# Six raw weight buffers and three pairs of split ones, in place of four and four

## The chip, the cores and the metric

The kernel runs on one core of one Trainium2 chip. The time is device microseconds from the first to the last instruction of the program, as a median over runs. Five engines work side by side, each with an instruction stream of its own: TensorE (PE in the profile; its weight loads are shown as PEld), VectorE (DVE), ScalarE (ACT), GpSimd (POOL) and SyncE (SP), which here issues nearly all loads from memory. They wait for one another through semaphores.

## The reference

The program is a forward pass over 256 tokens of width 1024 in fp32, through two blocks of two layers each. In outline:

```python
for l in range(2):                                # first block
    p = x @ w_in[l]
    h = concat(gmlp(p), diff_attention(p), pool(p)) @ w_out[l]
    x = layer_norm(ALPHA * x + h)
    f = swiglu(x, w1, w3, w2) if l == 0 else moe_ffn(x, router, w1, w3, w2)
    x = layer_norm(ALPHA * x + f)
for l in range(2):                                # second block
    z = rmsnorm(x) @ w_in_2[l]
    br = stack([sparse_attention(z), retention(z), conv_module(z)])
    x = x + sum(gate(z) * (br @ w_branch[l])) @ w_out_2[l]
    x = x + relu(rmsnorm(x) @ w_ff1[l]) ** 2 @ w_ff2[l]

def swiglu(x, w1, w3, w2): return (silu(x @ w1) * (x @ w3)) @ w2
def moe_ffn(x, ...):                              # top 2 of 8 experts, each a swiglu of width 3584
    return sum(gates[:, e] * swiglu(x, w1[e], w3[e], w2[e]) for e in range(8))
```

Every weight is read once. Nearly all the work is products of 256 tokens, or of the tokens that an expert has, with these weights.

## The kernel before

An fp32 product is made of three faster ones: a weight is split into a high part `wh` and a low part `wl`, an activation likewise, and high·high, low·high and high·low are summed in PSUM (line 84; line 945 for the experts).

**A unit** (`unit`, lines 166 to 212) is 2048 columns of weights on 128 partitions, 1 MB. It takes a raw buffer from the pool `pw` (tag "raw") and a buffer each for `wh` and `wl` from the pool `ph`. SyncE issues its load (line 188), ScalarE copies it into `wh` (line 165, which rounds), and VectorE subtracts `wh` from the raw weights into `wl` (line 166). There are 532 of these subtractions. A raw buffer is free for another load when the subtraction is done, a pair is free when TensorE's last product on it is done. A few other tensors take a raw buffer as well (the compression weights of the sparse attention, the merged branches).

**How units are called.** The dense products (`run_b`, `run_a`, `pipe`) load one unit ahead of the one that is multiplied. A dense unit has 24 products of 512 columns. At the head of a layer and in the output projection, two or three units are held at once, and all of them are multiplied with the first 128 tokens, then all with the second 128 (`tmajor`), while the normalization of one token tile runs.

**The experts** (`expert`, `moe`, `stream`) run from about 440 to 1470 us of the span and load 336 units, two to three ahead of their work. The branch that these inputs take, `few`, has two parts. In part 1, to about 840 us, three experts run interleaved: one with a full tile of 128 gathered tokens and a half one, so that a unit has 20 products, and two with a half tile of 64 tokens, so that a unit has 8. I call these heavy and light units. A round has 18 units, in runs of heavy ones and of light ones, and between the runs the products of the two up matrices are turned (`uT`, lines 992 and 999) and split for the down matrix (`uh`, `ul`, `uhl`). In part 2 one expert with one full tile runs at a time, 12 products to a unit, 6 units to a round.

**What sets the order.** The program is written as generators that are woven together, but each engine's final order is made by a scheduler at build time. It plays the program through with durations of its own and gives each engine the instructions in the order in which they could start there; an instruction that needs a buffer becomes possible when the buffer is free in that play. So the numbers of buffers (`bufs`, lines 402 and 403) move instructions on ScalarE, VectorE and, here and there, on TensorE and SyncE.

Of the kernel before, what the change touches and what calls it, by code (L numbers as in the profile page):

```python
# [75 lines left out]
class Acc:  # L76
    """a PSUM region that n matmuls accumulate in; fresh: the first one clears the bank"""
# [11 lines left out]
def weave(main, fill):  # L89
    """emit main; ("wait", us) in it is covered by that much tensor-engine work of fill, ("until", f) by  # L90
    what it takes to make f() true"""
    for kind, t in main:
        while kind == "until" and not t():
            next(fill)
        while kind == "wait" and t > 0:
            r = next(fill, None)
            if r is None:
                break
            if r[0] == "work":
                t -= r[1]  # L100
# [7 lines left out]
class Gated:  # L108
    """a generator that comes to a halt ahead of job n until ready()"""
# [16 lines left out]
def blend(a, b, every):  # L126
    """a, with a step of b emitted after each `every` us of it"""
    due = 0.0
    for r in a:
        yield r  # L130
        if r[0] == "work":
            due += r[1]
        while due >= every:
            due -= every
            next(b, None)


class Model:
# [29 lines left out]
    def unit(self, src, ks, c0, n, layout=None, scale=None):  # L168
        """rows of the k-tiles ks, columns c0.. of a weight, in two float32r parts [128, k, n]; scale: a factor
        [128, 1] for the rows of each k-tile"""  # L170
# [11 lines left out]
        else:  # L182
            i = 0
            while i < nk:
                j = i + 1
# [4 lines left out]
                i = j  # L190
# [5 lines left out]
        elif scale:  # L196
            i = 0
# [16 lines left out]
    def run_b(self, specs, x, tiles=(0, 1), tmajor=False, after=None):  # L214
        """token-layout products. specs: (src, ks, c0, n, {t: [(Acc, column slice)]}, layout);
        tmajor: all units for one token tile, then for the other; after[t]() is emitted behind tile t,
        after[t, i]() behind unit i of it"""
        nc = self.nc

        def emit(sp, u, t):  # L220
            h, l = u
            w = 0
            for kk, k in enumerate(sp[1]):
                xh, xl = x(k, t)
                for acc, cs in sp[4][t]:
                    acc.mm(nc, xh, h[:, kk, cs])
                    acc.mm(nc, xh, l[:, kk, cs])
                    acc.mm(nc, xl, h[:, kk, cs])
                    w += 3 * 0.000428 * (cs.stop - cs.start)
            return ("work", w)  # L230

        load = lambda sp: self.unit(*sp[:4], *sp[5:])
        if tmajor:
            us = [load(sp) for sp in specs]
            for t in tiles:
                for i, (sp, u) in enumerate(zip(specs, us)):
                    yield emit(sp, u, t)
                    if after and (t, i) in after:
                        after[t, i]()
                if after and t in after:  # L240
                    after[t]()
        else:
            nxt = load(specs[0]) if specs else None
            for i, sp in enumerate(specs):
                u, nxt = nxt, (load(specs[i + 1]) if i + 1 < len(specs) else None)
                for t in tiles:
                    yield emit(sp, u, t)

    def pipe(self, jobs):
        """token-layout products of one job after the other, units loaded ahead across them.  # L250
        jobs: (units, x, begin, end), units = [(src, ks, c0, n, layout, scale)] of n columns in all,
        begin() ahead of the products, end(banks) behind them; yields ("job", index) ahead of each"""
# [21 lines left out]
    def specs_b(self, src, nk, c0, n, tiles=(0, 1), layout=None, order=None, per=None,  # L274
                scale=None):
        """units and banks of out[t] = x[t] @ src[:, c0:c0+n]"""
# [7 lines left out]
    def run_a(self, src, c0, n, parts, x, nk=8, layout=None):  # L284
        """feature-layout product; parts: (bank, rows, column offset in bank, column offset in the unit)"""
# [19 lines left out]
    def feat(self, src, c0, nf, x, out):  # L305
        """nf tiles of 128 features, two to a bank: [128, f%2, tok]"""
# [3 lines left out]
    def to_feat(self, src, t, xh, xl):  # L310
        """src [128 tok, 1024] -> xh/xl[:, k, t*128:...] split transposed"""
# [20 lines left out]
    def bcast_row(self, dst, src):  # L332
        """DRAM vector [n] to all partitions of dst [128, n]"""
# [3 lines left out]
    def warm(self, func, after):  # L337
        """has the scalar engine's table for func loaded ahead of its use, once after [128, n] is there"""
# [6 lines left out]
    def rsqrt(self, v, eps):  # L345
        """v = (v + eps) ** -0.5 for a few columns, without a table of the scalar engine"""
# [33 lines left out]
    def project(self, src, orders, x, post, scale=None, first=None):  # L380
        """out = x @ src [., 1024]; the last three units go tile by tile, post(t, banks) behind each tile.
        orders: lists of k-tiles that make up units; first() is emitted behind the first products, self.early()
        ahead of the last"""
# [15 lines left out]
    def setup(self, ctx):  # L399
        tc, nc = self.tc, self.nc  # L400
        self.alpha = 4.0 ** 0.25
        self.pw = ctx.enter_context(tc.tile_pool(name="pw", bufs=4))
        self.ph = ctx.enter_context(tc.tile_pool(name="ph", bufs=4))
# [56 lines left out]
    def mix1(self, l, xt, tr1):  # L460
        """-> the generator of the output projection, begun. tr1() emits the transposes of the second token tile"""
# [156 lines left out]
    def attn1(self, qT, kT, v, bt, neglam, yth, ytl):  # L618
# [37 lines left out]
        def values(hp):  # L656
            """[token, (t, head of the pair, feature)]"""
# [118 lines left out]
    def ln_out(self, gen, g, b):  # L776
        """drains a projection into a layer norm; -> (transposed x, emitter of its second tile)"""
# [23 lines left out]
    def route(self, xt, rw):  # L801
        """by slot: gates, positions of the tokens (far off where they are not routed), expert, token count"""
# [51 lines left out]
        # slots: the experts by their number of tokens, most first. Of the 512 places, no more than three can  # L854
        # have over 128, and the last none over 64
# [49 lines left out]
    def gather(self, g, parts, xh, xl):  # L905
        """x^T of the tokens that the one-hots g[t] [128 tok, 256 or 512] pick, in two parts. parts: the
        destination [128, 8, n] of each part for columns of g, as (first column, n, high, low)"""
# [18 lines left out]
    def expert(self, tiles, w, acc):  # L926
        """the phases of acc[tok] += gate[tok] * swiglu of the gathered tiles, put back on their tokens: a list of
        (jobs, then), jobs = [(unit arguments, tensor-engine work on the unit, what follows it)]"""
# [4 lines left out]
        def mms(tile, src, k):  # L933
            """(stationary operand, part of the weights, rows of the product)"""
# [5 lines left out]
        def products(tile, src, ks, u, targets):  # L940
            """targets: (Acc, columns of the unit); ks: k-tiles of src"""
# [121 lines left out]
    def stream(self, jobs, ahead=2):  # L1063
        """emits jobs (unit arguments or None, work on the unit, what follows), units loaded ahead of their work"""
        queue, units = [], []

        def pull():
            """on to the next job with a unit, which is loaded"""
# [15 lines left out]
    def moe(self, xt, rw, w1, w3, w2, g2, b2):  # L1084
# [19 lines left out]
        def place(slots):  # L1104
            """slots: (slot, first position, half) of the tiles, in 512 columns -> tiles"""
# [43 lines left out]
        def phases(rounds):  # L1149
            """jobs of rounds of experts whose phases alternate; the last products of a phase follow the first of  # L1150
            the next"""
# [25 lines left out]
        def run(plan):  # L1177
            """plan: (groups of tiles to place, rounds of experts); a group is placed ahead of its first round"""
# [53 lines left out]
    def residual_norm(self, t, banks, dst):  # L1232
        """xn = x + banks; dst = rmsnorm(xn) * gamma, for token tile t"""
# [14 lines left out]
    def rms_out(self, gen, gamma, name=None):  # L1248
        """drains a projection into the residual and its norm; -> the norm by tile or, with a name, transposed and
        the emitter of its second tile"""  # L1250
# [28 lines left out]
    def mix2(self, l, xt, tr1):  # L1279
# [4 lines left out]
        # parameters that belong on partitions  # L1284
# [28 lines left out]
        # gated convolution input, in token layout first  # L1313
# [22 lines left out]
        # retention operands in token layout  # L1336
# [21 lines left out]
        def gates(n, c, dst):  # L1358
            """tanh of half the gate logits of branch n, columns 512 c.. -> dst() [128, t, 512]"""
# [8 lines left out]
        def branch(n, c, layout=None, scale=None):  # L1368
            """merged += 2 * gate * projection of branch n, columns 512 c.."""
# [21 lines left out]
        def turn(c):  # L1391
            """the transposed merged columns 512 c.. in two parts"""
# [88 lines left out]
    def ret_gate(self, w, tok, gr, ys):  # L1481
        """gr = 2 silu(g)"""
# [8 lines left out]
    def retention(self, r0, qk, vr, gr, dec, ys):  # L1491
# [20 lines left out]
        def values(t):  # L1512
            """[token, (head, feature)], normalized over the features"""
# [44 lines left out]
    def gelu_tanh(self, dst, src):  # L1558
        """0.5 x (1 + tanh(sqrt(2/pi) (x + 0.044715 x^3)))"""
# [40 lines left out]
    def nsa_in(self, l, w, full, par, fold, N):  # L1600
        """keys, values, gates and queries; tile j of the queries holds head j of both groups"""
# [6 lines left out]
        # windows of keys and values to compress; the positional part is one more window  # L1608
# [74 lines left out]
    def nsa(self, N, ys):  # L1683
# [62 lines left out]
        # compressed scores of all heads  # L1746
# [33 lines left out]
        # selection and window attention: with 256 tokens both see every earlier key  # L1780
# [110 lines left out]
```

## Time and profile before

| | |
|---|---|
| runs | 2375.16, 2378.10, 2379.86 us, median 2378.1 |
| profiled execution | span 2376.3 us; its own time beside the span is not given |
| TensorE busy | 2285.2 us (96%), 11444 products |
| VectorE busy | 1770.3 us (74%), of which `wl` of line 166: 1200.9 us in 532 |
| ScalarE busy | 1410.7 us (59%), of which `wh` of line 165: 1003.5 us in 532 |
| DMA | 585.10 MB, mean 246 GB/s |

The table adds up over stages with different limits, so it is read with the busy time by stretch. A product that is waiting in TensorE's pipeline counts as busy, so that its idle time is the surer number. Where an instruction in the order of time has a bracket behind it, its engine stood idle that long before it, and the bracket names what ended the wait.

### The profile page before, as it was taken

The numbers are of one execution on the slowest core, as the hardware profiler recorded it, in microseconds if no ns is written. First come the engines' busy times: TensorE is split into PE (matmuls) and PEld (weight loads), VectorE is DVE, ScalarE is ACT, GpSimd is POOL, SyncE is SP. The second block draws the span as 40 slices with busy tenths as digits, with TensorE's granted clock in tenths as the row PEclk, the third lists the DMA queues.
The fourth block names the chain that finished last, engine by engine and source line by source line (L and its number), as shares of the span: only waits on it lengthen the run. The fifth ranks groups of instructions, "written<-read, shape, count | busy, mean of one in ns | idle before, by whom it ended". The sixth has DMA issues, their size and how long they took to land. (4 is left out here: it accounts for less than half of the span.)

```text
span 2376.3 us, 29764 instructions
## 1 busy us (share of the span) xinstructions
PE 2285.2 (96%) x11444; PEld 1854.5 (78%) x11444; DVE 1770.3 (74%) x1907; ACT 1410.7 (59%) x1532; POOL 109.3 (5%) x154
## 2 busy tenths in 40 slices
PE   7999999799999989999999998899999999999998
PEld 6788886577777768887888776787888888888887
DVE  4665465798888998889888887898566459966653
ACT  5554354577777767677777775547554344764542
POOL 2100010100000000000000000100100001010000
PEclk9999999899999999999999999899999999999999
DMA  9456560699999989999999998553655554555552
GB/s 289 171 194 181 177 206 22 230 337 342 343 341 315 322 317 350 348 361 353 375 336 368 358 347 302 190 179 116 213 183 182 195 184 131 183 168 199 181 187 75
DMA packets 266967, 585.10 MB, mean 246 GB/s; under 512 B 10513, under 2 KB 21189, under 8 KB 266560
## 3 DMA queue, kind: packets, MB, share of 16 engines
q1 hardware_dynamic: 260880, 565.48, 68.7%
q0 software_dynamic: 5936, 17.64, 2.4%
q8 instruction: 91, 1.49, 0.3%
q14 instruction: 60, 0.49, 0.1%
HBM read 580.43 MB, written 2.64 MB: 245 GB/s over the span
## 5 line engine op out<-in xcount | busy, mean ns | idle before, releaser
L166 DVE TENSOR_TENSOR wl<-raw,wh 128x2048 fp32r<-128x2048 f32 (+2 forms) x532 | 1200.9, 2269 | 391.6 <-ACT wh L165 389.4
L165 ACT ACTIVATE wh<-raw 128x2048 fp32r<-128x2048 f32 (+2 forms) x532 | 1003.5, 1895 | 515.4 <-PE lin L84 145.1
L945 PE MATMUL lin<-wh,ring 128*128 128x512 f32 x1680 | 556.1, 392 | 0.0
L945 PE MATMUL lin<-wl,ring 128*128 128x512 f32 (+1 forms) x1008 | 399.0, 396 | 9.4 <-DVE wl L166 9.3
L945 PEld LDWEIGHTS lin<-wh,ring 128*128 128x128 f32 x1680 | 315.4, 188 | 81.2
L945 PEld LDWEIGHTS lin<-wl,ring 128*128 128x128 f32 (+1 forms) x1008 | 171.3, 170 | 63.2 <-DVE wl L166 23.2
L84 PE MATMUL lin<-wh,hh 128*128 128x512 f32 x352 | 142.0, 404 | 0.0
L84 PE MATMUL lin<-wl,hh 128*128 128x512 f32 x352 | 138.4, 393 | 2.3 <-DVE wl L166 2.3
L84 PE MATMUL lin<-wh,hl 128*128 128x512 f32 x352 | 138.0, 393 | 0.1
L945 PE MATMUL y<-wl,uh 128*128 128x512 f32 x336 | 107.6, 401 | 3.8 <-DVE wl L166 3.8
L1427 DVE SCALAR_TENSOR_TENSOR ro<-conv,ro 128x256 f32<-128x256 f32 x240 | 105.5, 474 | 0.4
L945 PE MATMUL y<-wh,ul 128*128 128x512 f32 x336 | 104.3, 391 | 0.0
L945 PE MATMUL y<-wh,uh 128*128 128x512 f32 x336 | 104.1, 390 | 0.0
L84 PE MATMUL lin<-wh,h2h 128*128 128x512 f32 x256 | 101.1, 395 | 0.0
L84 PE MATMUL lin<-wl,h2h 128*128 128x512 f32 x256 | 99.9, 390 | 0.2
L84 PE MATMUL lin<-wh,h2l 128*128 128x512 f32 x256 | 99.3, 390 | 0.2
L84 PE MATMUL lin<-wh,xah 128*128 128x512 f32 (+1 forms) x240 | 87.7, 366 | 0.7 <-ACT xah L165 0.6
L84 PE MATMUL lin<-wh,xal 128*128 128x512 f32 (+1 forms) x240 | 86.7, 364 | 0.0
L84 PE MATMUL lin<-wl,xah 128*128 128x512 f32 (+1 forms) x240 | 86.6, 361 | 0.0
L84 PEld LDWEIGHTS lin<-wl,hh 128*128 128x128 f32 x352 | 66.8, 190 | 16.1 <-DVE wl L166 3.2
L84 PEld LDWEIGHTS lin<-wh,hh 128*128 128x128 f32 x352 | 66.8, 190 | 15.7 <-issue 1.3
L84 PEld LDWEIGHTS lin<-wh,hl 128*128 128x128 f32 x352 | 66.7, 189 | 14.7 <-DVE hl L166 0.4
(543 smaller groups left out, 3781.0 us busy)
## 6 DMA issues: line engine op xcount, KB each, us to landing
raw<-in_moe_w SPq DMA_DIRECT2D x336, 1024.0 KB, 6.8
raw<-in_w_in SPq DMA_DIRECT2D x70, 1024.0 KB, 5.2
raw<-in_w_ff SPq DMA_DIRECT2D x64, 1024.0 KB, 5.2
raw<-in_ffn_w SPq DMA_DIRECT2D x32, 1024.0 KB, 5.1
raw<-in_w_out SPq DMA_DIRECT2D x12, 1024.0 KB, 8.2
raw<-in_w_branch SPq DMA_DIRECT2D x8, 1024.0 KB, 5.9
raw<-in_w_out SPq DMA_DIRECT2D x8, 512.0 KB, 8.3
raw<-in_w_branch SPq DMA_DIRECT2D x8, 512.0 KB, 6.4
```

Source lines behind the costliest of these rows:

```text
L84: nc.tensor.matmul(o, lhsT=lhsT, rhs=rhs, start=(self.i == 0 and self.fresh), stop=(self.i == self.n - 1), skip_group_check=True)
L165: self.nc.scalar.activation(h, src, AF.Copy)
L166: self.nc.vector.tensor_sub(l, src, h.bitcast(F32))
L945: nc.tensor.matmul(a.ap[:rows], lhsT=lhsT, rhs=u[part][:, kk, cs], start=(a.i == 0), stop=(a.i == a.n - 1), skip_group_check=True)
L1427: nc.vector.scalar_tensor_tensor(acc[:, f], uT[:, f, k:k + 256], cw[:, f, k:k + 1], acc[:, f], op0=OP.mult, op1=OP.add)
```

## The change

The pool of raw buffers gets six buffers in place of four, and the pool of split ones three of each tag in place of four. A raw buffer has 8 KB per partition and a pair 16 KB, so that the memory in use is the same. All else in the diff is comments that are taken out; no line number moves.

```diff
-        self.pw = ctx.enter_context(tc.tile_pool(name="pw", bufs=4))
-        self.ph = ctx.enter_context(tc.tile_pool(name="ph", bufs=4))
+        self.pw = ctx.enter_context(tc.tile_pool(name="pw", bufs=6))
+        self.ph = ctx.enter_context(tc.tile_pool(name="ph", bufs=3))
```

Every engine has the same instructions before and after, up to waits; what differs is the order. Two places show how.

The first is VectorE in part 1 of the experts, where a run of light units begins: `wl_4055`, `wl_4071`, `wl_4104` and `wl_4119` are the low parts of the first four light units of the run, `wl_4138` is that of the first heavy unit behind them, `ysum` the sum of a light expert's products, `ul` and `uhl` low parts of activations. Before:

```order
L166 TENSOR_TENSOR wl_4055<-raw_4053,wh_4054 128x2048
L980 TENSOR_TENSOR sa_3992<-sa_3992,lin_4016 128x512
L166 TENSOR_TENSOR wl_4071<-raw_4069,wh_4070 128x2048
L1022 COPY ysum_3382<-y_4059 128x512
L1022 COPY ysum_3382<-y_4060 128x512
L166 TENSOR_TENSOR wl_4104<-raw_4102,wh_4103 128x2048
L166 TENSOR_TENSOR ul_4091<-uT_4085,uh_4090 128x512
L166 TENSOR_TENSOR wl_4119<-raw_4117,wh_4118 128x2048
L166 TENSOR_TENSOR uhl_4099<-uT_4094,uhl_4099 128x4x64
L971 TENSOR_TENSOR sa_4131<-lin_4108,sa_4131 64x512
L166 TENSOR_TENSOR wl_4138<-raw_4136,wh_4137 128x2048
```

With the change:

```order
L980 TENSOR_TENSOR sa_3992<-sa_3992,lin_4016 128x512
L166 TENSOR_TENSOR wl_4055<-raw_4053,wh_4054 128x2048
L166 TENSOR_TENSOR wl_4071<-raw_4069,wh_4070 128x2048
L1022 COPY ysum_3382<-y_4059 128x512
L1022 COPY ysum_3382<-y_4060 128x512
L166 TENSOR_TENSOR ul_4091<-uT_4085,uh_4090 128x512
L166 TENSOR_TENSOR uhl_4099<-uT_4094,uhl_4099 128x4x64
L166 TENSOR_TENSOR wl_4104<-raw_4102,wh_4103 128x2048
L166 TENSOR_TENSOR wl_4119<-raw_4117,wh_4118 128x2048
L971 TENSOR_TENSOR sa_4131<-lin_4108,sa_4131 64x512
L166 TENSOR_TENSOR wl_4138<-raw_4136,wh_4137 128x2048
```

The multiplication of line 980 between the first two subtractions goes ahead of them, and `ul` and `uhl`, each of which stood behind a subtraction, go ahead of the third one, so that subtractions stand two by two.

The second is VectorE at the head of the dense feed-forward network, while the normalization ahead of it still runs (`r`, `st`, `mv`, lines 360 to 372): `wl_1090`, `wl_1096`, `wl_1102` and `wl_1194` are the low parts of its first four units, `xal` the low part of the first token tile. Before:

```order
L360 SCALAR_TENSOR_TENSOR r_1060<-x_86,prj_824 128x512
L166 TENSOR_TENSOR wl_1096<-raw_1094,wh_1095 128x2048
L166 TENSOR_TENSOR xal_1033<-tr_1034,xah_1032 128x4x128
L166 TENSOR_TENSOR xal_1033<-tr_1041,xah_1032 128x4x128
L362 BN_STATS st_1061<-r_1060 128x6
L360 SCALAR_TENSOR_TENSOR r_1060<-x_86,prj_826 128x512
L166 TENSOR_TENSOR wl_1102<-raw_1100,wh_1101 128x2048
L362 BN_STATS st_1061<-r_1060 128x6
L166 TENSOR_TENSOR wl_1194<-raw_1192,wh_1193 128x2048
```

With the change:

```order
L360 SCALAR_TENSOR_TENSOR r_1060<-x_86,prj_824 128x512
L166 TENSOR_TENSOR wl_1090<-raw_1088,wh_1089 128x2048
L166 TENSOR_TENSOR xal_1033<-tr_1034,xah_1032 128x4x128
L166 TENSOR_TENSOR xal_1033<-tr_1041,xah_1032 128x4x128
L362 BN_STATS st_1061<-r_1060 128x6
L360 SCALAR_TENSOR_TENSOR r_1060<-x_86,prj_826 128x512
L166 TENSOR_TENSOR wl_1096<-raw_1094,wh_1095 128x2048
L362 BN_STATS st_1061<-r_1060 128x6
L166 TENSOR_TENSOR wl_1102<-raw_1100,wh_1101 128x2048
```

Each unit's subtraction stands where the next unit's stood; that of the first unit stood farther ahead before, and that of the fourth, `wl_1194`, comes farther behind now.

## Rows read from the trace of the kernel before

**Rows 1.** The page, busy time, share of the span and instructions of TensorE.
```profile
PE 2285.2 (96%) x11444; PEld 1854.5 (78%) x11444; DVE 1770.3 (74%) x1907; ACT 1410.7 (59%) x1532; POOL 109.3 (5%) x154
```

**Rows 2.** Busy time by stretch (length, TensorE, weight loads, VectorE, ScalarE, GpSimd, clock, DMA).
```profile
140.00:200.00 60.00, 60.00 (x275) 49.85 (x274) 33.90 (x23) 29.61 (x23) 0.00 (x0) 1.00 0.62 203
440.00:840.00 400.00, 387.00 (x1766) 286.83 (x1764) 351.63 (x279) 298.07 (x266) 0.00 (x0) 1.00 0.95 333
840.00:1470.00 630.00, 619.76 (x2800) 502.73 (x2800) 554.96 (x365) 450.16 (x318) 0.00 (x0) 1.00 0.97 350
```

**Rows 3.** The page, issues of the experts' loads (count, size, median us to landing).
```profile
raw<-in_moe_w SPq DMA_DIRECT2D x336, 1024.0 KB, 6.8
```

**Rows 4.** Order of time, 512 to 531 (start, duration, engine, line, tiles, idle before and releaser).
```profile
512.13 1.90 ACT L165 ACTIVATE wh<-raw 128x2048 fp32r<-128x2048 f32 x1
...
515.20 2.29 DVE L166 TENSOR_TENSOR wl<-raw,wh 128x2048 fp32r<-128x2048 f32 x1
...
515.78 0.39 PE L945 MATMUL lin<-wh,ring 128*128 128x512 f32 x1
...
516.01 0.40 PE L945 MATMUL lin<-wl,ring 128*64 128x512 f32 x1
...
516.21 3.72 ACT L165 ACTIVATE wh<-raw 128x2048 fp32r<-128x2048 f32 x2 [2.18 <-PE lin L945]
...
520.37 1.28 DVE L1022 COPY ysum<-y 128x512 f32<-128x512 f32 x2
...
521.56 2.28 DVE L166 TENSOR_TENSOR wl<-raw,wh 128x2048 fp32r<-128x2048 f32 x1
...
523.76 0.68 DVE L166 TENSOR_TENSOR ul<-uT,uh 128x512 fp32r<-128x512 f32 x1
...
524.36 2.28 DVE L166 TENSOR_TENSOR wl<-raw,wh 128x2048 fp32r<-128x2048 f32 x1
...
525.20 0.39 PE L945 MATMUL lin<-wl,ring 128*64 128x512 f32 x1
...
526.56 0.41 DVE L166 TENSOR_TENSOR uhl<-uT,uhl 128x256 fp32r<-128x256 f32 x1
...
527.01 0.68 DVE L971 TENSOR_TENSOR sa<-lin,sa 64x512 f32<-64x512 f32 x1
...
527.73 2.29 DVE L166 TENSOR_TENSOR wl<-raw,wh 128x2048 fp32r<-128x2048 f32 x1
...
530.08 0.73 PE L945 MATMUL y<-wl,uh 128*128 128x512 f32 x2 [0.34 <-DVE wl L166]
```

**Rows 5.** Waits, 447 to 840 (engine and line, what for, total, times, longest).
```profile
PE y L945 <- DVE wl L166: 7.9, 16, 1.2
...
PE lin L945 <- DVE wl L166: 2.9, 6, 0.7
```

**Rows 6.** Waits, 840 to 1470.
```profile
ACT wh L165 <- DMA raw<-in_moe_w: 118.9, 120, 4.5
...
PE lin L945 <- DVE wl L166: 6.4, 13, 1.0
...
PE y L945 <- DVE wl L166: 1.1, 2, 0.9
```

**Rows 7.** Waits of SyncE's load queue, 840 to 1470.
```profile
SPq L188 <- DVE wl L166: 460.9, 195, 4.9
```

**Rows 8.** DMA, 840 to 1470 in 40 slices, GB/s.
```profile
GB/s 272 367 330 355 350 371 323 353 333 372 341 356 361 364 363 352 378 324 376 366 369 377 317 338 355 327 376 374 373 376 347 350 359 307 357 361 373 345 381 238
```

**Rows 9.** Order of time, 121 to 127, VectorE and TensorE.
```profile
125.64 2.28 DVE L166 TENSOR_TENSOR wl<-raw,wh 128x2048 fp32r<-128x2048 f32 x1
...
126.83 0.39 PE L84 MATMUL lin<-wl,xah 128*128 128x512 f32 x1
```

**Rows 10.** Order of time, 1582 to 1587, VectorE and TensorE.
```profile
1582.03 4.62 DVE L166 TENSOR_TENSOR wl<-raw,wh 128x1024 fp32r<-128x1024 f32 x4
...
1584.67 0.28 PE L84 MATMUL q<-hh,wl 128*128 128x256 f32 x1
```

## The prediction

> **What bounds the kernel now.** I read the busy shares first, then the busy time by stretch, then the list of waits in the two stretches where TensorE is not full, and last the order of time around one place of each kind. TensorE is busy 96% of the span [rows 1]. By stretch the picture splits in two. In a dense stretch TensorE works 60.00 of 60 us while the DMA engines are busy 0.62 [rows 2]: there a weight load that starts earlier can give nothing. In the mixture of experts TensorE lacks 400.00 − 387.00 = 13.0 us between 440 and 840, where three experts run interleaved (part 1), and 630.00 − 619.76 = 10.2 us between 840 and 1470, where one tile of tokens runs at a time (part 2); the DMA share is 0.95 and 0.97 [rows 2]. A weight load of 1 MB takes 6.8 us there [rows 3]. So all that a deeper load queue could save lies in these two stretches: 23 us at the very most, since TensorE's work stays the same. The granted clock is 1.00 in all three stretches [rows 2], so no term of the sum is a clock.
>
> A weight passes two rings. A raw buffer is taken when its load is issued and given back by VectorE's subtraction, and a pair (high, low) is taken by ScalarE's copy and given back by TensorE's last product on it. The change lengthens the first ring by two and shortens the second by one, so the price hangs on which ring is late where.
>
> **Part 1: the pair ring is the late one.** In each round the units run as heavy ones (20 products) and light ones (8 products). Before a run of light units the splits must be ahead, since a light unit is eaten in 8 × 0.23 = 1.84 us (a product follows the one before by 0.23 us, as 516.01 does 515.78) while VectorE needs 2.29 us for one subtraction [rows 4]. The same rows show how the ring stands: ScalarE's copy for the first light unit starts at 512.13, and the next one stands 2.18 us idle until 516.21, released by a product of TensorE. That is the pair ring with four pairs. With three, the copy of 512.13 itself must wait for that product, the end of the heavy unit three places back: the product starts at 516.01 and lasts 0.40, so it ends at 516.4. The copy then runs 516.4 to 518.35 (1.90 us as now, with 0.05 to start), and the subtraction can start at 518.4 where it started at 515.20: 3.2 us late.
>
> From there I walk VectorE in its new order, the one that stands under the change above: subtraction, subtraction, two sums, the two low parts of the turned activations, subtraction, subtraction, one addition, subtraction. Back to back these advance by 2.20, 2.20, 1.19, 0.60, 0.45, 2.20, 2.20, 0.72 us by the starts in rows 4, and the last takes 2.29. So the third subtraction ends at 518.4 + 2.20 + 2.20 + 1.19 + 0.60 + 0.45 + 2.20 = 527.2, and TensorE asked for it at 525.20 [rows 4]: a stall of 2.0 us. The fifth ends at 532.4, and the first heavy unit's low product, which ran at 530.08 after 0.34 us of waiting for VectorE [rows 4], has by then slipped to 532.1: 0.3 more. Nothing after it gives the 2.4 us back while TensorE is the bound; I take off the 0.3 us of the old wait that is contained in it and use 2.1 us. The place comes back in six rounds (from 507 to 840, some 55 us each), and the first round has a shorter one that I estimate at half: 6 × 2.1 + 1 = **+13.5 us**. Ends: if ScalarE and VectorE are ordered so that no stall results, and the loads no longer come late, all TensorE's waits for low parts in part 1 go, 7.9 + 2.9 = 10.8 us [rows 5]: −10.8. If the whole 3.2 us come through each time, 6 × 3.2 + 1 = +20.
>
> **Part 2: the load ring is the late one.** Here ScalarE waits 118.9 us in 120 places for a load [rows 6], and SyncE 460.9 us in 195 places for the subtraction that frees a raw buffer [rows 7]. Four buffers then turn once in a load of 6.8 us, a copy of 1.92 and a subtraction of 2.29, with small waits between: about 11.5 us for four units, 2.9 us each, where TensorE needs 12 products of 0.23 = 2.76 us. With six buffers the same turn gives 1.9 us per unit if the loads did not slow each other. TensorE's waits that come from it are small: 6.4 us for lin and 1.1 us for y [rows 6], 7.5 us in all, since much of the lateness is slack of ScalarE. The three pairs are long enough here: the copy starts when the unit three back ends, the low part is ready 1.92 + 2.29 + 0.04 = 4.25 us later, and it is wanted after two units, 5.52 us: 1.3 us over, from which one or two short VectorE operations of 0.68 us may be taken. I use **−6 us**: the waits of 7.5 us, less a fifth for what the loads lose by sharing. Ends: −10.2 (every idle microsecond of the stretch [rows 2]) and 0.
>
> What decides between them is whether the DMA engines can go faster than they do. In slices of this stretch they moved 378 and 381 GB/s, with a mean of 350 [rows 2, 8]; a round of six units is 6.29 MB, and TensorE's floor for it is 72 × 0.23 = 16.6 us or 380 GB/s. So the slices say: nearly. The Trainium skill, DMA: Bandwidth & Descriptors, section Where 436 GB/s comes from, says that for loads from HBM the memory's share per core of about 358 GB/s is what binds; by that a round could not come under 17.6 us, the term would be 0, and the sum 6 us higher. The slices of 378 and 381 do not agree with it for single stretches, the mean of 350 does not contradict it. The same page's section Bandwidth has 341 GB/s for 1 MB alone and 425 GB/s for 16 MB, so that more bytes in flight go faster; no run here shows that yet.
>
> **Outside the experts.** The raw buffers bring nothing, as said. The pairs cost where a split was just in time with four: as a rule each split now starts where the next unit's started before. At the start of the dense feed-forward network, the second unit's low part moves, by the order shown above, into the place of the third one's, which ran 125.64 to 127.92, and TensorE wanted it at 126.83 [rows 9]: 1.1 us. The turning of the second token tile, which had nine products of a fourth unit as cover, loses that too, which I put at 0.4. At the second layer's input the same estimate gives 1. In the second block's attention inputs the queries' low part is wanted at 1584.67 and the next unit's is made in the run of four half subtractions from 1582.03 that ends at 1586.65 [rows 10]: 2.0 us late if the order held, in both layers; the order changes there, and I take half, 2 × 1.0. Together **+4.5 us**, with ends of −2 (the shorter run of ScalarE leaves its queue freer) and +9 (every one of them doubled). If the cover of long dense runs were gone as well it would cost more; that is a rival below.
>
> **Sum.** +13.5 − 6 + 4.5 = +12 us. The profiled execution spans 2376.3 us, and its own time is not given apart; the median of the runs, 2378.1, lies 1.8 us above the span. 2376.3 + 12 + 1.8 = **2390 us**. A measurement of this kernel can tell about 0.2%, 4.8 us, from no change.
>
> **Rivals.** *Faster: the load ring was the whole story.* For it: SyncE's and ScalarE's waits in part 2 [rows 6, 7], and in part 1 a load share of 0.95 [rows 2]. If VectorE's new order, which brings two subtractions together and the small work after them, hides the ring of three in part 1, then the 7.5 us of part 2 and about half of part 1's 10.8 us go and nothing is added: 2378 − 13 = 2365; with part of the costs outside about 2368. It decides from the point where the first light unit's low part comes less than 3.2 − 2.0 = 1.2 us late. Against it: ScalarE's 2.18 us of waiting for TensorE with four pairs [rows 4].
>
> *No change.* Part 1 loses about 1 us per round, as it does if only the 2.0 us stall appears and half of it had been lost anyway further on in the round, and part 2 gives its 6 to 8: 2376 to 2382. For it: TensorE is full nearly everywhere [rows 1], and instructions are the same in kind and number.
>
> *Much slower: the third pair was cover at every change of layer.* Where a run of three units is held for both token tiles, three pairs leave none for the next job. If its whole split, 1.92 + 2.29 = 4.2 us, then lies open at the eight changes from mixer to feed-forward and back, that is 34 us; with half of them 17 us on top of my 12: about 2407. Against it: at these changes VectorE's normalization is what TensorE waits for, and one more split fits beside it.
>
> **How the numbers follow.** Forecast 0.60, own range 2383 to 2400. Much slower 0.10. No change 0.17. Faster 0.13. The slower side is 0.60 + 0.10 = 0.70. Range: 2371 to 2403; below lies most of the faster rival, above the greater part of the much slower one, together just under 2 in 10.
>
> **What the profile after would show.** Right: in part 1 TensorE waits about 2 us for VectorE's low part once per round, within the light units (the list of waits between 447 and 840 has about 23 us for it instead of 10.8), and a round is about 2 us longer; ScalarE's copy before them is released by a product of TensorE. In part 2 ScalarE's waits for loads fall from 118.9 us to under 40, its copies wait for TensorE instead, the stretch moves over 355 GB/s and is 5 to 8 us shorter. Outside, TensorE has a new wait of about 1 us near 127. Wrong: rounds of part 1 no longer than before, or part 2 not shorter with the same waits for loads; then the load rate was at its end. A new wait of 4 us at changes of layer would speak for the third rival.

## The result, and the profile after

The changed kernel takes 2400.39 us (median of 4 runs, 2399.01 to 2402.22) against 2378.28 us before (4 runs). The ratio is 1.0099, with a 95% interval of 1.0084 to 1.0113: slower, by 22 us or 1%. I had forecast 2390.

Of the page of the changed kernel, the busy times and the granted clock in 40 slices:

```profile
PE 2287.3 (95%) x11444; PEld 1860.5 (78%) x11444; DVE 1771.0 (74%) x1907; ACT 1410.9 (59%) x1532; POOL 97.4 (4%) x154
...
PEclk9999999899999999999999999999999999999999
```

Every engine has as many instructions as before [rows 1], and TensorE, VectorE and ScalarE are busy as long as before, to 2.1 us; of the 23.8 us that the span grew by, 21.7 are idle time of TensorE. (A slice is 60 us here, so that a short fall of the clock does not show in the second line.) To see where the time went, I cut both traces at the ends of TensorE's last product on certain units. Part 1 is cut here from the end of the dense feed-forward network, so it holds the routing as well.

| stretch | before | changed | difference | forecast |
|---|---|---|---|---|
| to the 60th unit (first layer, second mixer) | 416.9 | 416.5 | −0.4 | +2.5 |
| routing and part 1 | 431.2 | 457.2 | **+25.9** | +13.5 |
| part 2 | 624.5 | 612.3 | **−12.3** | −6 |
| second block, to unit 532 | 874.2 | 884.7 | **+10.5** | +2 |

The signs of the last three rows are as forecast, and each of their sizes is about double or more; the first row came out even, for a reason that is given below with the clock. The busy time by stretch, of before and then of the changed kernel, for part 1 and part 2 (length, TensorE with its number of products, weight loads, VectorE, ScalarE, GpSimd, clock, DMA share, GB/s):

```profile
416.90:848.13 431.23, 402.92 (x1857) 300.75 (x1858) 375.79 (x361) 310.79 (x282) 5.19 (x10) 0.98 0.91 319
848.13:1472.64 624.51, 614.64 (x2773) 497.99 (x2771) 547.13 (x353) 443.88 (x313) 0.00 (x0) 1.00 0.97 349
```

```profile
416.52:873.70 457.18, 411.71 (x1858) 303.56 (x1858) 376.10 (x361) 311.59 (x281) 5.23 (x10) 0.97 0.86 307
873.70:1485.95 612.25, 608.15 (x2772) 500.44 (x2771) 545.41 (x353) 443.39 (x313) 0.00 (x0) 1.00 0.97 352
```

In part 1 the DMA share fell from 0.91 to 0.86: the loads are ahead there, and nothing asks for them. In part 2 note that TensorE's busy time fell as well, 614.64 to 608.15 us for the same products.

**The place in part 1.** This is the same run of light units as in [rows 4]:

```profile
519.40 5.52 ACT L165 ACTIVATE wh<-raw 128x2048 fp32r<-128x2048 f32 x3 [1.33 <-PE lin L945]
...
521.35 4.49 DVE L166 TENSOR_TENSOR wl<-raw,wh 128x2048 fp32r<-128x2048 f32 x2 [0.96 <-ACT wh L165]
...
525.76 1.28 DVE L1022 COPY ysum<-y 128x512 f32<-128x512 f32 x2
...
526.59 0.47 PE L945 MATMUL lin<-wh,ring 128*128 128x512 f32 x1 [2.04 <-DVE ysum L1022]
...
527.89 2.28 DVE L166 TENSOR_TENSOR wl<-raw,wh 128x2048 fp32r<-128x2048 f32 x1
...
535.97 0.73 PE L945 MATMUL y<-wl,uh 128*128 128x512 f32 x2 [0.84 <-DVE wl L166]
```

ScalarE's copy waits for TensorE's end of the unit three back, and VectorE's two subtractions follow in a block, as the order said. But TensorE does not stop at the third subtraction, where I had put it. It stops before the first light unit, 2.04 us, for the sums of line 1022: these empty a PSUM bank that the first product's `lin` needs. They stand behind both subtractions, as they did before, and are now late with them: they begin at 525.76, where before they began at 520.37 [rows 4] and no one waited for them. The list of waits of part 1 of the changed kernel (what [rows 5] has for before):

```profile
ACT wh L165 <- PE lin L945: 68.5, 39, 3.4
...
ACT wh L165 <- PE y L945: 27.9, 15, 2.6
...
PE y L945 <- DVE wl L166: 13.8, 17, 1.3
...
PE lin L945 <- DVE ysum L1024: 10.2, 5, 2.0
...
PE lin L945 <- DVE wl L166: 2.2, 7, 0.7
...
PE lin L945 <- DVE ysum L1022: 2.0, 1, 2.0
```

Low parts and sums together: 28.2 us, against 10.8 us of before, so +17.4. A second place in each round adds a little to it, the run of light units further on. The same product with the change, and then before:

```profile
554.50 0.68 PE L945 MATMUL y<-wl,uhl 128*64 128x512 f32 x2 [1.25 <-DVE wl L166]
```

```profile
548.14 0.69 PE L945 MATMUL y<-wl,uhl 128*64 128x512 f32 x2 [0.78 <-DVE wl L166]
```

**The clock.** Behind some of these waits the granted clock falls to its lower level, 0.50 in the rows (1.2 GHz). After the second of the six waits for the sums, TensorE's products, and then the busy time in stretches of 2 us:

```profile
584.88 0.47 PE L945 MATMUL lin<-wh,ring 128*128 128x512 f32 x1 [2.04 <-DVE ysum L1024]
...
586.88 0.63 PE L945 MATMUL lin<-wl,ring 128*64 128x512 f32 x1
587.31 0.63 PE L945 MATMUL lin<-wh,ring 128*128 128x512 f32 x1
587.74 0.63 PE L945 MATMUL lin<-wl,ring 128*64 128x512 f32 x1
```

```profile
584.50:586.50 2.00, 1.62 (x7) 1.17 (x8) 2.00 (x5) 0.00 (x0) 0.00 (x0) 0.93 1.05 405
586.50:588.50 2.00, 2.00 (x6) 1.29 (x5) 1.96 (x1) 1.38 (x1) 0.00 (x0) 0.50 1.05 386
588.50:590.50 2.00, 2.00 (x8) 1.33 (x7) 1.44 (x1) 0.84 (x2) 0.00 (x0) 0.72 0.57 142
```

For about 3.4 us a product follows the one before by 0.43 us, not 0.23: 1.7 us lost. The profile of the changed kernel has such falls at 586, 767 and 866 in part 1 and at 1600, 1617 and 2043 in the second block, and one at 419 that costs 1.7 us more than that of before at 421; the profile of before has none of the six. Six times 1.7 is 10 us that stand in no list of waits.

The falls at 586 and 767 come right behind waits for the sums, at 584.88 and 766.3. Those at 419 and 866 are not shown to be the missing pair's. Of the kernels below that have four pairs in part 1, one has a fall as long as that at 419 (at 417, with loads into the pair tags), and two have one at the end of part 1, where 866 stands (at 840, with sums first in the kernel before and with the fifth raw buffer from the thirteenth unit on).

Before has a fall of 10.2 us, from 373 to 384, that the changed kernel has not. At 370 the changed kernel is 2.9 us behind, at the end of the first stretch 0.4 ahead; that is why this stretch of the table comes out even.

**Part 2** went as described. Waits there, changed kernel (before: [rows 6]):

```profile
ACT wh L165 <- PE lin L945: 58.8, 91, 2.5
...
ACT wh L165 <- PE y L945: 11.8, 16, 1.6
...
PE y L945 <- DVE wl L166: 1.2, 2, 0.7
...
PE lin L945 <- DVE wl L166: 0.9, 1, 0.9
```

ScalarE's waits for loads, 118.9 us, are gone from the list; its copies now wait for TensorE, 70.6 us, which is to say that the splits are as far ahead as three pairs let them be.

**The second block** has a wait that I had not named. ScalarE, then TensorE:

```profile
1594.44 1.06 ACT L165 ACTIVATE wh<-raw 128x1024 fp32r<-128x1024 f32 x1 [3.90 <-issue]
...
1596.20 2.84 ACT L165 ACTIVATE wh<-raw 128x1024 fp32r<-128x1024 f32 x2
1598.95 0.36 ACT L1640 ACTIVATE hs<-hid 128x256 f32<-128x256 f32 x1
```

```profile
1599.36 0.63 PE L1649 MATMUL hidT<-conv,hs 128*128 128x32 f32 x4 [1.51 <-ACT hs L1640]
```

A copy holds ScalarE idle for 3.9 us (I take it that it waits for a pair; the profile names no releaser, only "issue"), two more copies follow, and the small `hs` behind them comes 1.5 us late for TensorE. A fall of the clock comes right after it, at 1600. In the other layer the same wait of 1.5 us has one behind it at 2043.

### The profile page after: what moved, and what is told of

Read it like the earlier page. It is cut to its first block, busy times and chain, and to the rows that moved or that the text cites. A ratio compares the mean times of both kernels' runs of the same rounds, so it can differ in the third digit from the quotient of the medians.

```text
span 2400.1 us, 29799 instructions
## 1 busy us (share of the span) xinstructions
PE 2287.3 (95%) x11444; PEld 1860.5 (78%) x11444; DVE 1771.0 (74%) x1907; ACT 1410.9 (59%) x1532; POOL 97.4 (4%) x154
## 5 line engine op out<-in xcount | busy, mean ns | idle before, releaser
L945 PE MATMUL lin<-wh,ring 128*128 128x512 f32 x1680 | 559.0, 393 | 12.2 <-DVE ysum L1024 10.2
```

What stands on the lines that cost most here:

```text
L945: nc.tensor.matmul(a.ap[:rows], lhsT=lhsT, rhs=u[part][:, kk, cs], start=(a.i == 0), stop=(a.i == a.n - 1), skip_group_check=True)
```

## The experiments

The comparisons are ratios to the kernel before, run on the same chip.

**Pairs alone.** Four raw buffers, three pairs:

```diff
-        self.pw = ctx.enter_context(tc.tile_pool(name="pw", bufs=6))
+        self.pw = ctx.enter_context(tc.tile_pool(name="pw", bufs=4))
```

> Four raw buffers, three pairs: the half of the change that takes away. My theory after the result is that the two rings act apart: the pair ring costs 25 us in part 1 of the experts and about 11 us in the second block, the raw ring gives 12 us back in part 2. Then this kernel takes 2378 + 25 + 11 = 2414 us (2408 to 2420), part 1 is as long as with the change, and in part 2 ScalarE's waits for loads are near the 119 us of before. Rival: the six raw buffers are part of the cost (loads and subtractions that come earlier crowd part 1), and three pairs alone cost less than the whole change: 2385 to 2398 us. Second rival: part 2 is shorter because of the new order and not because of the raw buffers: 2400 us.

Measured: 2413.27 us (2408.53 to 2414.24), ratio 1.0153 (1.0136 to 1.0170). My sum was 2414. By stretch: part 1 455.7 us, as with the change; part 2 628.2 us, 16 us longer than with the change and 4 longer than before. In part 2 the waits for loads are there again:

```profile
ACT wh L165 <- DMA raw<-in_moe_w: 98.5, 104, 2.3
...
PE lin L945 <- DVE wl L166: 8.6, 15, 1.2
```

So part 1's cost is the pairs' and part 2's gain the raw buffers', and neither needs the other. The second block cost 5.8 us here and 10.5 with the change: one fall of the clock, not three, stands in this profile between 1600 and the last products, and TensorE's two waits for `hs` are not in it, so that these are not the pairs' alone.

**Sums first.** In the changed kernel:

```diff
-                            if f == 0:
-                                nc.vector.tensor_copy(o, p)
-                            else:
-                                nc.vector.tensor_add(o, o, p)
+                            with self.tc.high_priority():
+                                if f == 0:
+                                    nc.vector.tensor_copy(o, p)
+                                else:
+                                    nc.vector.tensor_add(o, o, p)
```

> The changed kernel, with the sums of the light experts' products (line 1022/1024 of before) given priority on VectorE, so that they stand ahead of the second subtraction of a run of light units. In the changed kernel TensorE waits 12.2 us in six places of part 1 for these sums, which free the PSUM bank that the next product needs. Theory: the bank is the place of the cost, and the granted clock falls after some of these waits; with the sums earlier 12 us of waits and up to 5 us of clock go: 2383 to 2389 us. Rival: the sums are only the first thing that is late; the third subtraction stands 2.2 + 1.2 + 2.2 us behind them in any case, TensorE waits 1.3 us for its low part instead of 2.0 us for the bank, and 0.7 us x 6 = 4 us go: 2394 to 2397 us.

Measured: 2393.61 us (2391.35 to 2395.91), ratio 1.0076 (1.0060 to 1.0093), just under the range that I gave the rival. The sums now stand behind the first subtraction. The waits for them are gone, and this is what the list of part 1 has in their place:

```profile
PE y L945 <- DVE wl L166: 14.8, 18, 1.3
PE lin L945 <- DVE wl L166: 9.0, 19, 1.0
```

Low parts rose from 16.0 to 23.8 us, while 12.2 us of sums went: in the list 4.4 us are saved. The stretch of part 1:

```profile
419.69:870.38 450.69, 408.23 (x1862) 299.96 (x1862) 377.90 (x363) 312.00 (x281) 5.22 (x10) 0.98 0.87 312
```

It is 6.5 us shorter than with the change, and its falls of the clock are as long as before, 6.8 us less than with the change. So what part 1 gained is the clock, and of the 4.4 us of waits nothing is left. The bank was the first thing late, not the cause. With it out of the way and no more clock lost than before, part 1 is still 450.7 − 431.2 = 19.5 us longer than before, though low parts cost only 23.8 − 10.8 = 13.0 us more in the list. The list leaves out lateness that stands in busy rows: counted from one product's start to the next, as far as that is over 0.23 us, the products on low parts lost 15.8 us before and 34.0 here, 18.2 more.

**Sums first, kernel before**, the same edit as a control:

> The kernel before with the same priority for the sums, as the control of the run of the changed kernel with sums first. With four pairs TensorE waits 10.8 us for low parts in part 1 and never long for a sum. Theory (the bank matters only when the sums are late): no change, 2376 to 2381 us. Rival (the order of VectorE's work around the sums costs in both kernels): 4 us or more less, under 2374 us.

Measured: 2375.73 us, ratio 0.9998 (0.9986 to 1.0011): no change. The place of the sums matters only once the splits are late.

**Loads into the pair tags, part 2 only.** The first try at the gain without the cost:

```diff
+        self.deep = self.deep + 1 if self.deep else 0
+        if self.deep % 3 == 2:
+            raw = self.ph.tile([128, 2048], F32R, tag="wh" if self.deep % 6 == 2 else "wl", name="raw").bitcast(F32)
+        else:
+            raw = self.pw.tile([128, 2048], F32, tag="raw", name="raw")
...
+                            self.deep = self.deep or (plan is few and i > 0)
```

> The kernel before, four raw buffers and four pairs, except that in part 2 of the experts every sixth unit's load goes to a buffer of the high tag and another sixth's to one of the low tag: there about six buffers are open to loads and about three pairs are left, part 1 and all the rest keep four and four. Theory: the gain in part 2 is the raw ring's, and is had without the cost elsewhere: 12 us less than before, 2364 to 2369 us, with ScalarE's waits for loads in part 2 under 20 us. Rival: the gain needs three pairs in fixed turns (the new order) or the loads in the pair tags wait as long as those of the raw tag: 2374 to 2382 us.

Measured: 2541.77 us, ratio 1.0702 (1.0685 to 1.0720). Both theories missed by far. SyncE's queue in part 2 shows why:

```profile
SPq L192 <- DVE wl L166: 326.7, 53, 7.7
SPq L192 <- PE lin L949: 94.9, 22, 5.5
SPq L192 <- PE y L949: 68.0, 27, 3.1
```

A load that goes into a buffer of a pair waits for TensorE's last product on it, and all loads behind it wait too, since the queue is in order. From 900 to 1500 us the kernel moves 278 GB/s, where part 2 of before moved 349. It says nothing on raw buffers alone, only that one ring should not serve two lives.

**A fifth raw buffer of its own, part 2 only.** Four pairs throughout; every fifth unit of part 2 is loaded into the memory of the light experts' sums (`ysum`), which are done by then:

```diff
-        raw = self.pw.tile([128, 2048], F32, tag="raw", name="raw")
+        self.deep = self.deep + 1 if self.deep else 0
+        e = {2: self.extra[0]}.get(self.deep % 5) if self.deep else None
+        if e is not None:
+            raw = e
+        else:
+            raw = self.pw.tile([128, 2048], F32, tag="raw", name="raw")
...
+        self.extra = [ysum.rearrange("p i d -> p (i d)")]
...
+                            self.deep = self.deep or (plan is few and i > 0)
```

> The kernel before with four pairs throughout, and in part 2 of the experts a fifth raw buffer: every fifth unit there is loaded into the memory of the light experts' sums, which are finished by then. Theory: part 2's gain is the load ring's. With five buffers the turn of 11.5 us gives a unit every 2.3 us, less than TensorE's 2.76, so nearly the whole gain of part 2 is there without the cost of the third pair: part 2 12 us shorter (four fifths of it at least), all else as before: 2364 to 2369 us, ScalarE's waits for loads in part 2 under 40 us. Rival: the loads share one rate, and a fifth load in flight only makes each one longer: 2373 to 2379 us, with loads of 8 us or more in place of 6.8.

Measured: 2366.18 us (2363.08 to 2369.76), ratio 0.9957 (0.9941 to 0.9972). In this kernel the first such load overwrites the sums before they are read, so that part of two experts' output is changed. The next run starts the fifth buffer at the thirteenth unit and computes all:

```diff
-        e = {2: self.extra[0]}.get(self.deep % 5) if self.deep else None
+        e = {2: self.extra[0]}.get(self.deep % 5) if self.deep > 12 else None
```

> As the run with a fifth raw buffer in part 2, but the fifth buffer is first used from the thirteenth unit of part 2 on, when the light experts' sums have been read. Theory: the gain stands, less what the first twelve units would have had (under 1 us): 2365 to 2370 us, and ScalarE's waits for loads in part 2 stay under 50 us. Rival: the earlier run was short because loads into the sums' memory stood ahead of work that they should have waited for: 2374 to 2380 us.

Measured: 2361.19 us (2359.74 to 2365.20, 5 runs), ratio 0.9936 (0.9922 to 0.9949): 15 us faster than the kernel before, more than I expected, and 39 us faster than the change. ScalarE's waits in part 2, and the busy time from 860 to 1440, this kernel and then before:

```profile
ACT wh L165 <- DMA raw<-in_moe_w: 16.2, 16, 4.8
```

```profile
860.00:1440.00 580.00, 578.78 (x2644) 477.98 (x2645) 517.25 (x335) 415.29 (x298) 0.00 (x0) 1.00 0.99 363
```

```profile
860.00:1440.00 580.00, 572.76 (x2591) 466.32 (x2592) 510.35 (x330) 416.39 (x293) 0.00 (x0) 1.00 0.98 354
```

In the same 580 us TensorE does 2644 products and not 2591; 53 of them, 0.23 us each, are 12 us. The waits for loads fall from 118.9 to 16.6 us with one more buffer (16.2, and 0.4 for loads into `ysum`). The rival, that loads share one rate that is at its end, falls: in this stretch a load takes 7.4 us (7.2 into `ysum`) and not 7.1, and the rate is higher all the same. (The 6.8 us of [rows 3] is the median over both parts.)

**Which half of the pair.** Five raw buffers, and three buffers for only one of the two parts, in the same memory:

```diff
-        h = self.ph.tile([128, 2048], F32R, tag="wh", name="wh")
-        l = self.ph.tile([128, 2048], F32R, tag="wl", name="wl")
+        h = self.ph.tile([128, 2048], F32R, tag="wh", name="wh", bufs=4)
+        l = self.ph.tile([128, 2048], F32R, tag="wl", name="wl", bufs=3)
```

> Five raw buffers, four for the high parts, three for the low ones, in the memory of before. Tells which half of the pair is the missing one. Theory: VectorE is late because its subtraction waits for a low buffer only through ScalarE's copy; with four high buffers ScalarE's copy runs ahead again and VectorE's subtraction waits itself for the third low buffer, in its own queue, with the sums behind it. Then part 1 is as long as with three pairs (2395 to 2402 us in all). Rival: the high part is the one that counts, since ScalarE is released by TensorE in the trace; then part 1 is nearly that of before and part 2 keeps its gain: 2370 to 2380 us.

and with the numbers 3 and 4 exchanged:

> Five raw buffers, three for the high parts, four for the low ones. If the high part counts alone (ScalarE's copy must wait for TensorE's end of the unit three back, and the subtraction follows the copy), this is as slow as three pairs: 2395 to 2402 us. If the low part counts alone: 2370 to 2380 us. If both count, this kernel and the one with four high and three low buffers are both near 2400 us.

Measured: four high and three low 2389.15 us (2387.24 to 2392.92), ratio 1.0059 (1.0039 to 1.0078); three high and four low 2400.70 us (2398.58 to 2405.53), ratio 1.0104 (1.0084 to 1.0125). Parts 1 and 2 of the one and of the other:

```profile
417.44:856.47 439.03, 405.15 (x1858) 302.40 (x1858) 375.07 (x361) 308.99 (x282) 5.19 (x10) 0.98 0.88 317
856.47:1468.54 612.07, 607.94 (x2773) 500.40 (x2771) 543.01 (x353) 431.70 (x312) 0.00 (x0) 1.00 0.97 354
```

```profile
422.02:876.81 454.79, 408.86 (x1858) 301.58 (x1858) 375.98 (x361) 311.67 (x281) 5.20 (x10) 0.97 0.85 305
876.81:1488.90 612.09, 607.95 (x2772) 500.24 (x2771) 545.29 (x353) 443.34 (x313) 0.00 (x0) 1.00 0.97 354
```

In part 1 the missing high buffer alone costs all that the missing pair costs (454.8 us, against 457.2 with the change); the missing low buffer alone costs 8 us (439.0 against 431.2), of which 1.7 are a fall of the clock at 849, the place of the fall at 866 above. Neither theory of the first run had it quite; the second run lies where the high part alone was to put it. The high part is the one that counts, as the trace's releaser of ScalarE's copies says, but the low part is not free. Part 2 is 612.1 us in both, as with six raw buffers: the fifth gives the whole gain, the sixth nothing that can be seen. That four high and three low do not end nearer to before is the second block, which took 887.5 us there, 3 us longer than with the change; I did not follow it further.

## Why the prediction was right or wrong, point by point

**Part 1: the mechanism held, the term was mis-sized, 13.5 us for 25.9.** The step that failed is "6 × 2.1 + 1 = +13.5". The ring of three makes the split late as I had said: ScalarE's copy starts at 519.40 behind TensorE's last product on the unit three back, and the subtraction 1.95 us later. What followed from it cost more than the walk had. Without the falls of the clock it is 19.1 us: the seven rounds (cut at every 216th product of line 945) grew by 2.4 to 3.0 us each, where I had 2.1, and the first one by 2.6, where I had put 1 by estimate. Three things were left out of the walk.
- The walk followed VectorE to the third subtraction and never asked what else hung on the work between. The sums in it free a PSUM bank; TensorE stopped for them first, 2.04 us, in the place of the 2.0 us that I had priced for the low part. This moved the stall and hardly its size: with the sums first, part 1 is still 19.5 us longer than before, without a further fall of the clock. (That the list of waits has 13.0 us there, nearly my term, is no proof of it: from start to start it is 18.2.)
- I priced one place in a round. In the second run of light units the wait of before, 0.78 us, became 1.25.
- I wrote that no term of the sum is a clock, because the clock was 1.00 in the rows of before. In part 1 of the changed kernel's profile falls of the clock take 6.8 us more than before, four times 1.7. Two of the four, 3.4 us, come right behind waits for the sums; the other two stand where kernels with four pairs have one as well, so that the record does not show them to be the change's.

**Part 2: −12.3 us for −6, beyond the end of −10.2.** The steps that failed are "the waits of 7.5 us, less a fifth" and, for the end, "TensorE lacks 630.00 − 619.76 = 10.2 us". Idle time of TensorE was taken for all that there is to gain. The waits for low parts fell from 7.5 to 2.1 us, but the busy time of the stretch fell too, by 6.5 us for the same products. From start to start, the products on low parts came 15.6 us late before and 7.4 with the change (each step as far as it is over 0.23 us), so that part of their lateness stands in rows that count as busy. What was lost there was to be read from the time of the stretch against its products, not from its idle time. That the pairs are long enough in part 2 held: ScalarE waits 70.6 us for them and TensorE 2.1 us for low parts. The rate was 352 GB/s, and I had named over 355 as a sign.

**The rate of the loads.** The slices of 378 and 381 GB/s were the better guide [rows 8]. The fifth raw buffer holds 363 GB/s over 580 us, so the limit of about 358 GB/s per core that the Trainium skill names (DMA: Bandwidth & Descriptors, section Where 436 GB/s comes from) does not agree with this kernel on one core. The same page's section Bandwidth has a higher rate for a transfer of 16 MB (425 GB/s) than for one of 1 MB (341 GB/s). That more bytes in flight go faster, which I took from this, agrees: 363 GB/s, with loads of 7.2 to 7.4 us, against 354 with 7.1.

**Outside the experts: +10.1 us in all for +4.5.** In the first block the head of the dense network cost 2.7 us (to unit 49), for 1.5, and the next layer's head 1.1, for 1.0; the fall of the clock at 373, which only before has, hides it in the table. In the second block the low part of the queries, which I had priced, was ready early enough; what was late was `hs`, 1.5 us, twice, and I had not looked at what is queued behind a copy that waits on ScalarE. Half of the 10.5 us there is clock, three falls of 1.7. Most of what is left are three waits of about 1 us at changes of layer (1768, 1953 and 2210), where the low part of the activations now stands behind a subtraction.

**The sum.** The terms were off by +12.4, −6.3 and +5.6 us. That 2390 lay within 11 us of the measured time is partly luck: the error in part 2 made up for half of that in part 1.

**The rivals.** The gain from raw buffers is real (the faster rival's half) and the order did not hide the ring. No whole split of 4.2 us lay open at the changes of layer, where the new waits of TensorE are about 1 us at most; the much slower rival fell.

## What to carry to other kernels

Two rings in a row are two questions: for each stretch, find which one the copy waits for (a load, or a product), and give the memory to that one there. Here four pairs and a fifth raw buffer, lent where its memory was idle, had the gain of the change without its cost. When a wait is added on an in-order engine, list everything queued behind it and who needs each, the small instructions and those that free a bank above all; and take the bound of a gain from the time of the stretch, not from the idle time of an engine whose rows stretch when it waits.

## What the runs showed of the hardware that was not expected

Six waits of TensorE, alike in length (2.0 us, in six rounds of part 1), had different ends: after the second and the fifth the clock was at 0.50 for some 3.4 us, after the first it stayed at full speed. The two other runs that have the six waits (pairs alone; three high, four low) have a fall behind two of them as well, but not the same two: the first and the fifth, the first and the fourth. The two waits for `hs` had falls behind both in the changed kernel, behind one with three high and four low, and behind none with the sums first. What decides it the rows do not show. The cost of one fall, 1.7 us, is nearly that of the wait ahead of it, so such a wait in a kernel like this costs about 2 or about 4 us, and which of the two can't be read off before it is run.
